# Values in a phase of their own ahead of attention, by seven block products of eight, and output weights from head 13 on

## The chip, the cores and the metric

The kernel runs on one core of one Trainium2 chip. The metric is device time in microseconds (us) for one execution. PE is the matmul engine (TensorE), DVE is VectorE, ACT is ScalarE, POOL is GpSimd, and SP (SyncE) is the engine whose queue issues nearly all DMAs here.

## The reference, cut to what matters

A two-layer encoder trunk over 1024 tokens of width 1024, in float32. Layer 0 mixes tokens with a gated MLP (gMLP) and then has a convolutional feed-forward network. From the residual stream behind it one shared key and value is projected. Layer 1 is chunked attention with 16 heads of 64 against that key and value, again followed by a feed-forward network, and a last normalization.

```python
h = h + gmlp_mixer(rmsnorm(h, a_norm_g[0]), ...)
h = h + conv_ffn(rmsnorm(h, f_norm_g[0]), ...)
kv = rmsnorm(h, kv_norm_g) @ w_kv                 # shared keys and values
k_shared, v_shared = jnp.split(kv, 2, axis=-1)
# chunk_attention: chunks of 64, the own chunk and 8 before it
q = (rmsnorm(h, b_norm_g[0]) @ w_q) * HEAD_DIM ** -0.5
sc = einsum('bqhd,bkhd->bhqk', qb, kb) + bias     # per head, clipped relative positions
p = softmax(where(valid, sc, -1e30))
o = einsum('bhqk,bkhd->bqhd', p, vb)
h = h + o @ w_o
h = h + conv_ffn(rmsnorm(h, f_norm_g[1]), ...)
return rmsnorm(h, final_norm_g)
```

## The kernel before, in words

**Arithmetic.** Every large matmul is done as three: each operand is split into a high part, rounded to the matmul's number format, and a low part, the rest. The products high x high, high x low and low x high are summed (`products`, L174; the three matmuls are on L181, L184 and L188). `split` (L137) makes the parts: ACT casts the high one (L139), DVE or POOL subtracts for the low one (L140). A matmul takes a stationary block of 128x128 and 512 moving columns. `proj` (L169) runs `products` over all 8 blocks of the contraction: 24 matmuls for a result of 128x512.

**Seven products of eight.** The feed-forward networks and the output projection of layer 0 multiply 2x2 blocks with seven block products. Sums of blocks of the weights (S1 to S4) and of the activations (T1 to T4) stand in for single blocks; the tables `LEFT` and `RIGHT` (L302) say which product takes which. `block_sum` (L383) makes a sum, `down` (L913) is the second matmul of a feed-forward network, in 77 steps of 12 matmuls, and adds its results to the residual h.

**Order of work.** PE's order is written out by hand. A clock `tick` (L57) counts matmul time as the code is written, and `put_off` (L66) keeps a piece of work pending until that clock has passed a given number of microseconds, so that it falls between other matmuls. The other engines, SP's queue of DMAs among them, get their order from a scheduler, but for some stretches (in `down` ACT, DVE and SP are by hand up to step 24). An engine works through its own order strictly, and an instruction that waits holds up what stands behind it. Pools of buffers set when a tile can be written again.

**Normalization.** `norm` (L284) is called when `down(0)` has finished a half t of the tokens: `norm_tile` (L257) multiplies a block of h by the row of reciprocal root mean squares into y and splits it into `yh`, `yl`. These are the moving operands of the projections.

**Projections.** The heads come in pairs, 8 pairs p, each 128 features. With the token halves t there are 2 x 24 matmuls for q, k and v of each pair. Pair 0 has its own code right behind `down(0)` (`w2`, `ps2`, and a joint loop on L1128). For pairs 1 to 7 the generator `heads` (L1169) yields after every matmul, in the order q, k, v, and the attention loop takes some matmuls of it per step as fill. `operand` (L1070) moves a result out of PSUM: ACT and DVE make `thi` and `tlo` for q and k. `stage` (L1095) brings them with six DMAs of 64 rows into the operands QE, QS, KM, KS of a head (c is the head's place in its pair; SP queue; L1103). `constant_rows` (L1060) fills the other 64 rows of QE and KM from an input of constants by way of a buffer `e` (DMA L1065, ACT copy L1066). For v, `operand` copies PSUM to `vT`, and `transpose_v` (L1179) turns it on PE (`vtr`, L1182), four 128x128 pieces at a time; ACT and DVE split it into VH and VL, for c=1 by way of a piece that `stage_v` (L1190) moves with two DMAs.

**Attention.** For head hd, `Max` loads the head's bias (L1200), forms the row maxima of scores plus bias from matmuls `mx` (L1210, L1217; DVE reads them with the bias on L1213 and L1219), and its `row` transposes them on PE (`mr`, L1226) and puts them into a row of QE by DMA (L1230). `Head.score` is the score matmul `st` (L1256, L1258), which reads that row. `Head.value` is `po` (L1286 on). The loop has 16 heads of 8 steps. Ahead of it `START` = 58 matmuls of `heads` run, and the first head's maxima are put off by 4.0 us and 0.8 us more for each block, the row by 11.2 us. The number `n` of fill matmuls per step is 12 or 6, for pair 0 (144-58)/16, about 5.4 (3, then 6, in head 13; 5 in heads 14 and 15).

**Output projection.** `output` (L1383) multiplies by w_o; before the change it is used as fill from head 14 on for six of the eight blocks m, and the rest follows after the loop (`open_h("b")`, L1468 on). Sixteen DMAs from ACT's queue save h in `hsave[1]` behind pair 0 (L1138); `hr` reads them back at the end.

## Time and profile before

| | us |
|---|---|
| median of 3 runs | 2132.54 (2130.45 to 2134.04) |
| the profiled execution | 2131.62 |
| its span, first to last instruction | 2129.5 |
| PE busy | 2116.1 |
| DVE busy | 1546.9 |
| ACT busy | 1066.3 |
| POOL busy | 744.6 |

The span is 2.1 us shorter than the execution's own time. Instants below are microseconds from the span's start. `down(0)` ends at 926.9, pair 0's projections fill the stretch to 963, attention runs from there to 1404, and the output projection to 1477. An engine's busy time says how long it had an instruction in hand, not whether something waited for it; the chain of waits tells that. The granted clock of PE was 1.00 in all stretches shown.

### The profile page before, as it was taken

The page shows a single profiled execution, that of the slowest core. Times are in us where ns is not written, and L with a number is a line of the kernel's source. Part 1 is how long each engine was busy: PE and PEld are TensorE (multiplying, and loading weights), DVE is VectorE, ACT ScalarE, POOL GpSimd, SP SyncE. Part 2 cuts the span into 40 slices and gives each one's busy share as a digit, 9 for nine tenths or more (in the row PEclk, how much of TensorE's full clock was granted, in tenths as well). Part 3 has the DMA queues.
Part 4 walks back from the last instruction along what each step waited for, and adds up shares of the span by engine and source line. Part 5 has one row for each costly group of instructions (what it writes and reads, how often), then busy time and mean ns, then how long its engine had stood idle before and what let it go on. Part 6 is the DMA issues. An engine that isn't in the chain of part 4 may idle for free.

```text
span 2129.5 us, 28843 instructions
## 1 busy us (share of the span) xinstructions
PE 2116.1 (99%) x9944; PEld 1771.8 (83%) x9944; DVE 1546.9 (73%) x2313; ACT 1066.3 (50%) x1878; POOL 744.6 (35%) x528
## 2 busy tenths in 40 slices
PE   9999999999999999999999999999999999999998
PEld 8888878888888888878888888888888888888887
DVE  4188789888888857676565665665988888885576
ACT  6333555554445544555555555643645544454443
POOL 1075644332334412054444543421323323342020
PEclk9999999999999999999999999999999999999999
DMA  7267733454445966635555455762244545578653
GB/s 252 80 203 253 242 104 99 139 188 140 172 162 194 299 254 219 238 110 139 132 135 127 127 127 135 186 214 108 79 148 135 187 134 174 164 278 303 213 188 129
DMA packets 181450, 367.86 MB, mean 173 GB/s; under 512 B 42908, under 2 KB 43292, under 8 KB 181304
## 3 DMA queue, kind: packets, MB, share of 16 engines
q1 hardware_dynamic: 177128, 358.47, 52.6%
q10 hardware_dynamic: 4176, 7.55, 1.0%
q8 instruction: 78, 1.28, 0.3%
q14 instruction: 68, 0.56, 0.1%
HBM read 233.12 MB, written 103.40 MB: 158 GB/s over the span
## 4 chain that ended last, share of the span: by engine, by line
PE 93%; DVE 4%; ACT 1%; issue 1%; DMA 0%; POOL 0%; SPq 0%; DVEq 0%; POOLq 0%; ACTq 0%
PE up L995 10%; PE gate L995 10%; PE up L375 7%; PE up L377 7%; PE up L380 7%; PE gate L375 5%; PE gate L380 5%; PE gate L377 5%; PE vps L510 4%; PE qkv L184 4%; PE qkv L181 4%; PE qkv L188 4%; PE ups L181 1%; PE po L1290 1%; PE st L1256 1%; PE po L1288 1%
## 5 line engine op out<-in xcount | busy, mean ns | idle before, releaser
L140 DVE TENSOR_TENSOR wlo<-raw,whi 128x512 fp32r<-128x512 f32 (+1 forms) x395 | 346.5, 883 | 179.7 <-ACT whi L139 179.3
L139 ACT CAST whi<-raw 128x512 fp32r<-128x512 f32 (+1 forms) x395 | 245.1, 623 | 281.1 <-PE gate L995 197.4
L375 PE MATMUL up<-yh,whi 128*128 128x512 f32 x688 | 268.1, 390 | 0.7 <-ACT gate L886 0.6
L377 PE MATMUL up<-yh,wlo 128*128 128x512 f32 x688 | 267.8, 389 | 0.0
L847 POOL TENSOR_TENSOR h<-a 128x512 f32<-128x512 f32 x44 | 82.0, 1864 | 403.3 <-DVE a L839 390.7
L1270 POOL TENSOR_TENSOR pl<-p,ph 128x640 fp32r<-128x640 f32 (+4 forms) x128 | 159.7, 1250 | 173.2 <-ACT ph L1269 128.0
L375 PE MATMUL gate<-th,whi 128*128 128x512 f32 x496 | 192.9, 389 | 0.0
L377 PE MATMUL gate<-th,wlo 128*128 128x512 f32 x496 | 192.9, 389 | 0.0
L380 PE MATMUL up<-yl,whi 128*128 128x512 f32 x688 | 184.2, 389 | 0.0
L375 PEld LDWEIGHTS up<-yh,whi 128*128 128x128 f32 x688 | 129.2, 188 | 28.9 <-ACT gate L886 2.0
L380 PEld LDWEIGHTS up<-yl,whi 128*128 128x128 f32 x688 | 129.1, 188 | 27.3 <-POOL yl L140 0.5
L377 PEld LDWEIGHTS up<-yh,wlo 128*128 128x128 f32 x688 | 129.2, 188 | 26.6
L140 DVE TENSOR_TENSOR yl<-raw,yh 128x512 fp32r<-128x512 f32 x172 | 143.1, 835 | 8.5 <-ACT yh L139 8.1
L184 PE MATMUL qkv<-yh,wlo 128*128 128x512 f32 x336 | 134.3, 400 | 0.0
L380 PE MATMUL gate<-tl,whi 128*128 128x512 f32 x496 | 132.8, 389 | 0.2 <-DVE tl L140 0.2
L181 PE MATMUL qkv<-yh,whi 128*128 128x512 f32 x336 | 132.4, 394 | 0.0
L139 ACT CAST whi<-S 128x512 fp32r<-128x512 f32 x160 | 99.2, 620 | 66.2 <-PE up L380 60.3
L140 DVE TENSOR_TENSOR wlo<-S,whi 128x512 fp32r<-128x512 f32 x160 | 130.6, 817 | 0.0
L995 PE MATMUL up<-yl,whi 128*128 128x512 f32 (+1 forms) x312 | 120.6, 387 | 0.0
L995 PE MATMUL gate<-yh,wlo 128*128 128x512 f32 (+1 forms) x312 | 120.4, 386 | 0.0
L995 PE MATMUL up<-yh,whi 128*128 128x512 f32 (+1 forms) x312 | 120.4, 386 | 0.0
L995 PE MATMUL up<-yh,wlo 128*128 128x512 f32 (+1 forms) x312 | 120.3, 386 | 0.0
(307 smaller groups left out, 5263.7 us busy)
## 6 DMA issues: line engine op xcount, KB each, us to landing
raw<-in_f_win SPq DMA_DIRECT2D x88, 512.0 KB
gT<-h SPq DMA_DIRECT2D x88, 256.0 KB
h<-in_f_wdown SPq DMA_DIRECT2D x44, 512.0 KB
dS<-h SPq DMA_DIRECT2D x88, 256.0 KB
raw<-dS SPq DMA_DIRECT2D x40, 512.0 KB
raw<-gT SPq DMA_DIRECT2D x40, 512.0 KB
gB<-a SPq DMA_DIRECT2D x66, 256.0 KB
raw<-in_f_wdown SPq DMA_DIRECT2D x30, 512.0 KB
```

Of the source, the lines that this page charges most:

```text
L139: behind[S] = S.copy(hi, src)
L140: return eng.tensor_tensor(lo, src, f32(hi), op=ALU.subtract)
L181: nc.tensor.matmul(ps, wh[:, k, :], xs[k][0], start=k == 0, stop=False)
L184: nc.tensor.matmul(ps, wl[:, k, :], xs[k][0], start=False, stop=False)
L188: nc.tensor.matmul(ps, wh[:, k, :], xs[k][1], start=False, stop=k == last)
L375: nc.tensor.matmul(ps, wh[:, k, :], xs[k][0], start=first and k == 0, stop=False, skip_group_check=True)
L377: nc.tensor.matmul(ps, wl[:, k, :], xs[k][0], start=False, stop=False, skip_group_check=True)
L380: nc.tensor.matmul(ps, wh[:, k, :], xs[k][1], start=False, stop=k == 3, skip_group_check=True)
L510: nc.tensor.matmul(ps, a, b, start=k == i == 0, stop=k == KD - 1 and i == 2)
L847: G.tensor_tensor(B[n], x, B.get(y) if isinstance(y, str) else y, op=ALU.subtract)
L995: nc.tensor.matmul(ps[:, cs], w[:, ms], x[:, cs], start=q == i == 0 and p in (1, 6, 5, 4), stop=q == NP - 1 and i == 2, skip_group_check=True)
L1270: marks[2] = G.tensor_tensor(pl[:, :n], pf[:, :n], f32(ph[:, :n]), op=ALU.subtract)
```

## The change

Values no longer take part in the fill. Behind `down(0)` a phase `values()` computes V for all heads with tokens on partitions, by the seven block products in the order 1, 2, 3, 6, 7, 5, 4, each for four token tiles m and four blocks of the contraction, 12 matmuls for a tile. Products 2 and 7 go on in the PSUM bank of products 1 and 6. The weights' sums (`value_sums`) are made on POOL during `down(0)`, at its steps 28, 37, 46 and 55, and go through DRAM (`va`); the gain is applied to them there. `norm` now scales h in place and makes the activations' sums T1 to T4 in place behind it; the T operands are split as they are needed (`tee`). The results are split and stored in DRAM (`vd`), and `stage_v` reads each head's piece, 64 columns, straight into VH and VL, while `vT`, the transposes and `constant_rows` ahead of pair 0 go. The phase stops twice (`yield`) for pair 0's q and k, t=0 behind product 1 and t=1 behind product 3. Their results stay in PSUM until the phase is over; only then come `first`, `stage(0, ...)`, `constant_rows` for c=0 and c=1 (two buffers, tag "o"), and `stage(1, ...)`.

The fill of attention is then only q and k (672 matmuls, `START` = 75 of them ahead of the loop), spread evenly over the 13 x 8 steps of heads 0 to 12. Heads 13 to 15 are filled with the output projection, 4 matmuls a step and 5 in every fourth; blocks m = 2 to 5 are first done for five of the eight k and added to `hr`. The weights w_o are asked for at steps 100 to 116. The put-off of the first maxima is 6.5 + 0.8 b, that of the row 14.0. The stores of h to `hsave[1]` move into `down(0)`. Core of the diff:

```diff
-START = 58
+START = 75
...
-    def norm(h, acc, t, gain, ys):
+    def norm(h, acc, t, X):
...
             def tile_k(k):
-                ys[t][k] = norm_tile(h[k][:, halves[t]], bc, k, gain, npl)
-            for k in range(KD):
-                put_off(0.9 * k, lambda k=k: tile_k(k))
+                y = h[k][:, halves[t]]
+                V.tensor_tensor(y, y, bc, op=ALU.mult)
+                X[f"B{1 + k // 4}{1 + t}"][k % 4] = b = new_y()
+                split(*b, y, V if k % 2 else G)
+
+            def sums(k):
+                (y11, y12), (y21, y22) = [[h[i][:, hs] for hs in halves] for i in (k, k + 4)]
+                V.tensor_tensor(y11, y12, y11, op=ALU.subtract)
+                V.tensor_tensor(y12, y22, y12, op=ALU.subtract)
+                V.tensor_tensor(y22, y22, y11, op=ALU.subtract)
+                G.tensor_tensor(y21, y21, y22, op=ALU.subtract)
...
                 behind["h"] = V.tensor_tensor(x, ps[:, cs], x, op=ALU.add)
+                if not l:
+                    (nc.scalar if t else nc.sync).dma_start(hsave[1][m + 4 * (p in (5, 4)), :, halves[t]], x)
...
+    def value_sums(k):
+        rows = [vs.tile([P, T], F32, tag="vr", name="vr") for _ in range(2)]
+        for j in range(2):
+            nc.sync.dma_start(rows[j].rearrange("p (m c) -> p m c", c=P), value_rows(0, k + 4 * j))
+            c = C_KVG + k + 4 * j
+            G.tensor_tensor(rows[j], rows[j], cc[:, c:c + 1].broadcast_to([P, T]), op=ALU.mult)
+        A = {f"A{n + 1}{j + 1}": rows[j][:, halves[n]] for n in range(2) for j in range(2)}
+        for n in va:
+            nc.sync.dma_start(va[n][k], block_sum(A, n, lambda: vs.tile([P, H], F32, tag="vS", name="vS", bufs=8), G))
...
+    def values():
...
+        def out(n, t, m, src, eng=V):
+            hi, lo = (npl.tile([P, H], F32R, tag="acc", name=a, bufs=4) for a in ("vh", "vl"))
+            split(hi, lo, src, eng)
+            for d, a in zip(vd, (hi, lo)):
+                nc.sync.dma_start(d[4 * t + m, :, halves[n]], f32(a))
...
+            elif p == 5:
+                out(1, 1, m, added(ps, s1[m]), G)
+                out(0, 1, m, added(ps, x[m]))
+            else:
+                out(1, 0, m, added(ps, s1[m]))
...
+        for n, (p, m) in enumerate(steps):
+            if p in (2, 6) and m == 0:
+                yield
+            if todo:
+                weight(*todo.pop(0))
+            if n + 2 < len(steps):
+                tee(*steps[n + 2])
+            if p not in (2, 7):
+                bank[m] = psA("v")
...
+            for k, (xh, xl) in enumerate(operand(p, m)):
+                wh, wl = wv[p, k]
+                for i, (a, b) in enumerate(((xh, wh), (xh, wl), (xl, wh))):
+                    nc.tensor.matmul(bank[m], a, b, start=p not in (2, 7) and k == i == 0, stop=k == 3 and i == 2,
+                                     skip_group_check=True)
+                    tick()
+            whole(p, m, bank[m])
...
+        for t, _ in enumerate(values()):
+            ys[t] = X["B11"] + X["B21"] if t == 0 else X["B12"] + X["B22"]
+            for what in "qk":
+                if t:
+                    ps2[what, 1] = psS("qk")
+                proj(ps2[what, t], w2[what], ys[t])
...
+    for t in range(2):
+        for what in "qk":
+            first(what, t)
+        stage(0, halves[t])
...
-        constant_rows(1, lambda: b2.tile([P, H], F32, tag="o", name="e"))
         for c in range(2):
+            constant_rows(c, lambda: b2.tile([P, H], F32, tag="o", name="e"))
...
-            order = [(p, what) for p in range(1, KD) for what in ("q", "k", "v")]
+            order = [(p, what) for p in range(1, KD) for what in "qk"]
...
+        def stage_v(hd):
+            for dst, a in zip((VH, VL), vd):
+                nc.sync.dma_start(f32(dst[hd % 2][:, :, rows[hd % 2][0]]),
+                                  a[:, :, hd * 64:(hd + 1) * 64].rearrange("b p c -> p b c"))
...
-        stage(1, halves[0])
+        for hs in halves:
+            stage(1, hs)
+        stage_v(0)
         mx = Max(0)
         for b in range(NB):
-            put_off(4.0 + 0.8 * b, lambda b=b: mx.block(b))
-        put_off(11.2, mx.row)
+            put_off(6.5 + 0.8 * b, lambda b=b: mx.block(b))
+        put_off(14.0, mx.row)
...
+            if s < ends:
+                n = left * (s + 1) // ends - left * s // ends
+            else:
+                n = 4 + (s % 4 == 3)
...
+            if i == LAG + 1 and hd + 1 < NH:
+                stage_v(hd + 1)
```

More of the change, by code (lines that the diff above doesn't have):

```diff
@@ L172, in proj, with products @@
             pass
-    def products(ps, w, xs, ks, last):
+    def products(ps, w, xs, ks, last, first=0):
         wh, wl = w
@@ L911, in ffn, with down @@
         return gs, ds
-    def down(l, gs, ds, hold, after):
+    def down(l, gs, ds, hold, after, aside={}):
         wd = f_wdown[l].rearrange("(q e p) c -> p q e c", e=2, p=P)
@@ L1040, in trunk @@
+    raws["ctx"].close()
+    npool_ctx.close()
+    h_ctx.close()
     open_raw(3)
@@ L1383, in output, with load_hr @@
         def output(todo):
-            for m, load, bank in todo:
-                w = load()
+            for m, ks, bank in todo:
                 ps = bank("wo")
-                yield from products(ps, w, os_[0], range(LAST), None)
-                outs.append((m, w, ps))
-        outs, head, waiting, ws = [], None, [], {}
-        loads = [0, 2, 8, 10, 11, 12]
+                yield from products(ps, ws[m], os_[0], ks, ks[-1] if ks[-1] < LAST - 1 else None, ks[0])
+                if ks[-1] < LAST - 1:
+                    V.tensor_tensor(hr[m], ps, hr[m], op=ALU.add)
+                else:
+                    outs[m] = ps
+        def load_hr(i):
+            place = f32(bt.tile([P, T], F32R, tag=("thi", "tlo")[i % 2], name="hr"))
+            for j in range(2):
+                hr[2 * i + j] = place[:, halves[j]]
+                with tc.issue_after(behind["row"].ins):
+                    nc.sync.dma_start(hr[2 * i + j], hsave[1][2 * i + j, :, halves[0]])
+        outs, head, waiting, ws = {}, None, [], {}
+        loads = {100: 2, 102: 3, 106: 4, 109: 5, 112: 0, 116: 1}
+        left = 2 * 6 * KD * LAST - early
+        ends = 13 * NB
         mid, end = {2: (1,), 3: (3,), 4: (5,), 5: (7,)}, {1: (0,), 2: (2,), 3: (4,), 4: (6,)}
```

235 lines of the change are left out of this document (118 added, 117 removed).

## The prediction

> **What bounds the kernel now.** I read the page first: the span, the busy shares and the chain that ended last.
>
> ```profile
> span 2129.5 us, 28843 instructions
> PE 2116.1 (99%) x9944; PEld 1771.8 (83%) x9944; DVE 1546.9 (73%) x2313; ACT 1066.3 (50%) x1878; POOL 744.6 (35%) x528
> PE 93%; DVE 4%; ACT 1%; issue 1%; DMA 0%; POOL 0%; SPq 0%; DVEq 0%; POOLq 0%; ACTq 0%
> ```
>
> PE is busy for 99% of the span and holds 93% of the chain. So a matmul that goes away counts in full, and so does every microsecond in which PE is made to wait. "Mean ns of one" is no price for a matmul, since matmuls overlap. The price is the pitch from start to start, which an unbroken piece of the chain of waits gives (72 matmuls of 128x512), and for the small transposes the timeline of PE (start, length, instruction):
>
> ```profile
> 55.66 16.35 PE vps L510 x72
> ...
> 962.66 1.03 PE L1182 MATMUL vtr<-ident,vT 128*128 128x128 f32 x8
> 963.45 0.47 PE L181 MATMUL qkv<-yh,whi 128*128 128x512 f32 x1
> ...
> 967.89 0.22 PE L1210 MATMUL mx<-km,qe 128*128 128x128 f32 x1
> ...
> 975.49 0.27 PE L1226 MATMUL mr<-ident,mb 128*8 128x128 f32 x1
> ...
> 978.82 0.28 PE L1256 MATMUL st<-qe,km 128*128 128x256 f32 x1
> ```
>
> 16.35/72 = 0.227 us for a 128x512 matmul; (963.45 - 962.66)/8 = 0.099 us for a transpose. The last three rows time the entry to attention, used below: first maximum product (mx) at 967.89, its row transpose (mr) at 975.49, first score (st) at 978.82.
>
> The busy time by stage (the end of down(0), pair 0's projections, the entry, heads 0, 1, 13 and 15) shows how much room the other engines have:
>
> ```profile
> core 0: us, PE busy (x) PEld busy (x) DVE busy (x) ACT busy (x) POOL busy (x), PEclk, DMA share, GB/s
> 873.00:926.90 53.90, 53.90 (x241) 44.39 (x240) 37.62 (x54) 28.11 (x51) 13.29 (x9) 1.00 0.47 156
> 926.90:963.00 36.10, 35.34 (x160) 28.71 (x159) 22.25 (x35) 18.61 (x35) 16.59 (x15) 1.00 0.50 147
> 963.00:979.00 16.00, 16.00 (x82) 13.38 (x81) 11.86 (x33) 5.85 (x12) 2.75 (x2) 1.00 0.74 196
> 979.00:1000.50 21.50, 20.89 (x114) 17.96 (x114) 13.63 (x38) 13.38 (x29) 13.63 (x11) 1.00 0.26 65
> 1000.50:1022.20 21.70, 21.70 (x125) 19.17 (x124) 11.71 (x37) 13.19 (x30) 12.84 (x12) 1.00 0.44 109
> 1338.00:1358.00 20.00, 20.00 (x115) 17.68 (x115) 10.63 (x34) 12.81 (x27) 10.03 (x9) 1.00 0.88 238
> 1381.00:1404.00 23.00, 22.25 (x118) 19.10 (x118) 19.10 (x29) 16.03 (x34) 10.23 (x9) 1.00 0.59 186
> ```
>
> The entry (963 to 979) costs PE nothing today: 16.00 of 16.00 us busy.
>
> **What goes.** The V projections of pairs 1 to 7 are part of three groups of 336, and the transposes are one of 64:
>
> ```profile
> L188 PE MATMUL qkv<-yl,whi 128*128 128x512 f32 x336 | 95.1, 396 | 0.0
> L1182 PE MATMUL vtr<-ident,vT 128*128 128x128 f32 x64 | 9.5, 273 | 0.4 <-ACT vT L1092 0.4
> ```
>
> A third of 3 x 336 is V, 336 matmuls, and pair 0 has 48 more: 384. The phase does 7 x 4 x 12 = 336. So 48 matmuls go, 48 x 0.227 = 10.9 us, and 64 transposes, 64 x 0.099 = 6.3 us: **-17.2 us**. With them go vT's copies and splits from PSUM, on engines with room.
>
> **What moves at no price, and its cover.** 597 of the 672 q,k fills are spread over 104 steps, 5.7 a step; heads 0 and 1 hold 5.4 a step today, and head 1 has PE busy for 21.70 of 21.70 us. Heads 13 to 15 get 4.25 output matmuls a step; head 13 now averages 4.5 (3, then 6) without a gap, and head 15 loses 0.75 us at 5. If that cover fails I expect up to 1 us a head, 3 us in all; I take 0. The 16 stores of h go from ACT's queue to SP and ACT within down(0), behind the adds that make x; PE waits for none of them. The row that each head's value needs from DRAM is asked for in the head before, about 13 us ahead (five of eight steps of a 21.7 us head). The wait of PE at the second half's statistics (36.10 - 35.34 = 0.76 us) may stay or go; I count nothing.
>
> **The block sums in down(0): 8 gain products and 16 sums on POOL.** Prices: the sums of down's own h, and a gain product beside DVE splits (POOL's timeline, then DVE's):
>
> ```profile
> L847 POOL TENSOR_TENSOR h<-a 128x512 f32<-128x512 f32 x44 | 82.0, 1864 | 403.3 <-DVE a L839 390.7
> ...
> 976.25 4.20 POOL L159 TENSOR_TENSOR raw<-raw,cc 128x1024 f32<-128x1024 f32 x2 [17.35 <-DMA raw<-in_w_q]
> ...
> 962.61 0.69 DVE L140 TENSOR_TENSOR wlo<-raw,whi 128x512 fp32r<-128x512 f32 x1 [1.50 <-ACT whi L139]
> ...
> 976.35 2.35 DVE L140 TENSOR_TENSOR wlo<-raw,whi 128x512 fp32r<-128x512 f32 x1 [0.91 <-ACT whi L139]
> ...
> 979.22 1.78 DVE L140 TENSOR_TENSOR wlo<-raw,whi 128x512 fp32r<-128x512 f32 x1
> ```
>
> POOL gets 16 x 1.86 + 8 x 2.10 = 46.6 us more. A split that takes 0.69 us alone took 2.35 and 1.78 beside POOL: 2.75 us lost in 4.20 of POOL, so 46.6 us could cost DVE 30.5. They stand in 36 of down's steps of 12 matmuls, 98 us; DVE's slack there is 1 - 37.62/53.90 = 30%, 29.6 us. It just fits. I take 0 here, and +1 (0 to 3) for the step p=3 of the phase, where eight DVE ops and the POOL halves stand between two uses of a bank.
>
> **The new wait: the entry to attention.** Before, constant rows, bias and half of pair 0's staging go out on SP while PE still projects pair 0. SP's order there (e: constant rows; km, qe, qs, ks: staging of q and k; thi, tlo: their halves):
>
> ```order
> L1065 DMA e<-in_consts 64x512 x2
> L1200 DMA bias<-in_bias 128x512 x2
> L1103 DMA km_8618<-thi 64x512
> L1103 DMA qe_8616<-thi 64x512
> L1065 DMA e<-in_consts 64x512 x2
> L1103 DMA qs_8617<-thi 64x512
> L1103 DMA qe_8302<-thi 64x512
> ```
>
> After the change, the same place of SP:
>
> ```order
> L1182 DMA e<-in_consts 64x512 x2
> L1213 DMA km_9394<-thi 64x512
> L1213 DMA qe_9392<-thi 64x512
> L1182 DMA e<-in_consts 64x512 x2
> L1213 DMA qs_9393<-thi 64x512
> L1213 DMA qs_9393<-tlo 64x512
> L1182 DMA e<-in_consts 64x512 x2
> L1213 DMA ks_9395<-tlo 64x512
> L1213 DMA ks_9395<-thi 64x512
> L1182 DMA e<-in_consts 64x512 x2
> ```
>
> Ahead of it now stand 24 stores of V pieces and the 12 stagings of head 0; behind it six stagings, two loads of V, and only then the bias. And it is all late, since ACT makes thi only behind the last V split (vh: V's high half, c: the sum it is cast from):
>
> ```order
> L139 CAST vh_9259<-c_9257 128x512 [waits DMAHW7_49,DVE_49,Activation_49]
> L139 CAST vh_9280<-c_9278 128x512 [waits DMAHW1_49,DVE_49,Activation_49]
> L1199 ACTIVATE thi_9354<-qk_8386 128x512
> L1202 CAST thi_9358<-qk_8387 128x512 [waits PE_49]
> L1199 ACTIVATE thi_9354<-qk_8800 128x512
> L1202 CAST thi_9358<-qk_8825 128x512
> ```
>
> What moved: pair 0's eviction went from beside its projections to behind the whole phase. On PE, before:
>
> ```order
> L188 MATMUL qkv<-yl,whi 128x512 x3
> L1210 MATMUL mx<-km_8304,qe_8302 128x128
> L188 MATMUL qkv<-yl,whi 128x512 x3
> L1210 MATMUL mx<-km_8304,qe_8302 128x256
> L188 MATMUL qkv<-yl,whi 128x512 x2
> ```
>
> and after:
>
> ```order
> L181 MATMUL qkv<-yh,whi 128x512
> L1286 MATMUL mx<-km_9352,qe_9350 128x128
> L184 MATMUL qkv<-yh,wlo 128x512
> L181 MATMUL qkv<-yh,whi 128x512
> L184 MATMUL qkv<-yh,wlo 128x512
> L1286 MATMUL mx<-km_9352,qe_9350 128x256
> ```
>
> The first mx now stands 31 fills behind the last V matmul (before, 19 behind the transposes), and st 75 fills behind it instead of 58. The prices, from SP's timeline, ACT's and DVE's:
>
> ```profile
> 952.25 1.28 SPq L1065 DMA_DIRECT2D e<-in_consts  x2
> 953.57 1.27 SPq L1200 DMA_DIRECT2D bias<-in_bias  x2
> ...
> 957.84 1.14 SPq L1065 DMA_DIRECT2D e<-in_consts  x2
> ...
> 966.00 0.59 SPq L1103 DMA_DIRECT2D km<-thi  x1
> ...
> 969.20 0.59 SPq L1103 DMA_DIRECT2D ks<-thi  x1
> ...
> 970.66 0.67 SPq L1192 DMA_DIRECT2D vl<-vlo  x1
> ...
> 998.99 0.39 SPq L1200 DMA_DIRECT2D bias<-in_bias  x1
> ...
> 960.63 1.33 ACT L1066 CAST km<-e 64x512 fp32r<-64x512 f32 x2 [0.34 <-DMA e<-in_consts]
> ...
> 968.14 0.29 DVE L1213 CUSTOM_DVE_ANT_0 junk<-mx,bias 128x128 f32<-128x128 f32 x1 [1.84 <-DMA km<-thi]
> ...
> 975.21 0.23 DVE L1221 SCALAR_TENSOR_TENSOR mb<-ma,cc,mb 128x6 f32<-128x6 f32 x1
> ```
>
> One issue: (969.20 - 966.00)/5 = 0.64 us. One constant row: 957.84 to 960.63, 2.8 us, and a cast of 0.6, 3.4 in all. The maxima on DVE: 968.14 to 975.44, 7.3 us; from mr to st 3.3.
>
> Let T be the end of the last V matmul. Its sum, cast and split: 0.7 + 0.6, T+1.3. Then SP issues 14 rows up to the last staging of head 0, 9.0 us: the first constant row leaves at X = T+10.3 at best. The V pieces have four buffers; a cast, a store and its landing are some 4.5 us for a pair of pieces, two pairs at once, so 2.2 us a pair where p=5 makes one each 1.36 us: eight pairs fall 6.9 us behind and p=4 (2.72 us a pair) gives 2 back. X is T+10 to T+15; I take 12.5. The four pairs of constant rows share two buffers, so each waits for the cast of the last: 3 x 3.4 = 10.2. Two rows, six stagings, two loads: 10 x 0.64 = 6.4, and the bias leaves at X+16.6, lands at +19.4 (2.8, as a constant row), DVE is through at +26.7, st can start at X+30. PE gets there by itself at 75 x 0.227, and 2.2 for the mx (before: 978.82 - 963.45 - 58 x 0.227): T+19.2. **Wait: X + 10.8, +23.3 us (21 to 26).** Behind the waiting mx stand all fills, in PE's own order.
>
> The sum: -17.2 + 23.3 + 1.0 = +7.1 on the profiled execution's 2131.62 us (span and 2.1 us around it). That execution lies 0.92 below the median of the runs, 2132.54, so I forecast **2139.6 us**; its own range is -17.2 + 21 + 0 to -17.2 + 26 + 3, 2136 to 2144.
>
> The Trainium skill, DMA: Bandwidth & Descriptors, "Issuing engines are not separate DMA queues", says the time a sequencer takes to start a DMA is usually small beside the DMA itself. The rows above say 0.64 beside 2.8, which is small for one and not for 24 in a row; by the rule the sum would be that of the second rival.
>
> **Rivals.**
> 1. *The issues are shorter in quiet* (0.39 us, as the bias at 998.99): X = T+1.3+5.5, then 10.2 + 3.9 + 2.8 + 7.3 + 3.3 = T+34.3; wait 15.1, 2132.5 - 17.2 + 15.1 + 1.0 = 2131. For it: DMA was 74% busy when 0.64 was seen. Against it: the constant rows at 952.25 also took 0.64 each.
> 2. *Issues cost nothing, only landings do* (SP is done before its rows are needed): 1.3 + 10.2 + 2.8 + 7.3 + 3.3 = T+24.9, wait 5.7, 2132.5 - 17.2 + 5.7 + 1.0 = 2122. Against it: between 966.00 and 969.20 SP had six stagings in a row and each took its 0.64.
> 3. *Slower still: DVE becomes the bound of down(0).* If a DVE op beside POOL always loses POOL's whole time, DVE loses 46.6 us against 29.6 of slack: 17 us more, 2157; half of it 2148. It decides once DVE's busy time in a step passes 2.72 us. For it: 2.35 against 0.69. Against it: 2.75 lost in 4.20, not all. That it would lose all of it is what the Trainium skill, SBUF — State Buffer, "Who interferes with whom", says of an op with two SBUF inputs beside a GpSimd op that reads SBUF: whoever comes second blocks fully.
>
> That the work doesn't go isn't open: PE's order has 48 matmuls and 64 transposes less.
>
> **Chances.** Forecast 0.48; rival 1 0.18; rival 2 0.20; rival 3 0.08; 0.06 for a full gain with hardly a wait, below 2120. About 0.2% (4.3 us) is what a measurement can tell from no change: 2128.3 to 2136.8. Forecast: 0.46 slower, 0.02 same. Rival 1: 0.04 faster, 0.11 same, 0.03 slower. Rival 2 and the rest: faster. Rival 3: slower. Faster 0.30, same 0.13, slower 0.57. The range of 8 in 10 runs from 2120 (0.06 below) to 2148 (0.08 above).
>
> **What would show it.** Right: the last V matmul to the first st takes about 42 us with PE idle for some 23 of them, first in front of mx (releaser ACT km<-e), then of the later mx (DVE junk, behind DMA bias), then of st (DMA qe<-mr); elsewhere 17 us less of PE. Wrong: PE busy through the entry (rival 2), or gaps in down(0) with DVE as releaser (rival 3); a pitch other than 0.227 in the phase would upset the gain.

## The result and the profile after

| | kernel before | changed kernel |
|---|---|---|
| median of 4 runs beside each other (range) | 2131.81 us | 2197.49 us (2194.22 to 2200.13) |
| ratio, 95% interval | | 1.0306 [1.0288, 1.0324] |
| profiled execution: time, span | 2131.62, 2129.5 us | 2200.13, 2198.4 us |

The change makes the kernel slower by 3.1%. The forecast, 2139.6 us, had the sign; 2197.49 lies far above its range (2120 to 2148). In the experiments two kernels had one execution each that was far slower (row_step5 7525.49 us, best_hr 3525.64); their ratios and ranges are of the other three. The first rows of the changed kernel's page, to be held against those of before in the prediction:

```profile
span 2198.4 us, 28916 instructions
PE 2124.1 (97%) x9832; PEld 1770.0 (81%) x9832; DVE 1591.9 (72%) x2354; ACT 1075.4 (49%) x1879; POOL 802.0 (36%) x560
PE 83%; DMA 6%; DVE 6%; issue 2%; POOL 1%; SPq 1%; ACT 1%; DVEq 0%; POOLq 0%; ACTq 0%
```

112 matmuls went (9944 to 9832), as forecast, but PE is idle for 2198.4 - 2124.1 = 74.3 us where it was idle for 13.4, and DMA, which had 0% of the chain, now has 6%. Busy time by stage shows where (length, then PE busy; the stages are the second half of down(0), the value phase, the entry, heads 0 to 12, heads 13 to 15, the end of the output projection):

```profile
core 0: us, PE busy (x) PEld busy (x) DVE busy (x) ACT busy (x) POOL busy (x), PEclk, DMA share, GB/s
744.00:931.00 187.00, 182.39 (x793) 148.50 (x792) 146.83 (x172) 92.56 (x165) 74.84 (x44) 0.99 0.79 269
931.00:1037.40 106.40, 105.86 (x469) 87.17 (x468) 79.73 (x108) 44.09 (x77) 39.22 (x27) 1.00 0.38 129
1037.40:1087.00 49.60, 24.33 (x90) 19.11 (x90) 14.37 (x35) 11.14 (x20) 9.30 (x10) 0.69 0.70 186
1087.00:1386.00 299.00, 285.84 (x1529) 247.53 (x1527) 173.02 (x499) 179.78 (x376) 155.40 (x135) 0.98 0.61 149
1386.00:1464.00 78.00, 68.08 (x354) 58.73 (x355) 46.86 (x115) 43.86 (x93) 32.57 (x29) 0.96 0.65 181
1464.00:1486.00 22.00, 14.43 (x57) 11.27 (x56) 16.18 (x28) 8.17 (x15) 2.91 (x3) 0.80 0.39 130
```

The value phase is as forecast: PE waits 106.40 - 105.86 = 0.54 us in all of it. Idle time is in five places: 4.6 us in down(0), 25.3 at the entry, 13.2 in heads 0 to 12, 9.9 in heads 13 to 15, 7.6 behind the last score. The clock column tells of a second cost: 0.69 at the entry, where it was 1.00 before. Busy time doesn't count that. So I worked out for each stage the excess: over all neighbouring matmuls, the distance from start to start, less the median distance that the same form has in the kernel before. It holds idle time and lowered clock alike (us, in profiled executions; heads 0 to 12 run from the first score to the row transpose mr of head 13; "rest" is up to 700 us, the value phase and all behind the output projection):

| kernel | down(0) from 700 us | entry | heads 0-12 | heads 13-15 | behind the last score | rest | sum |
|---|---|---|---|---|---|---|---|
| before | 0.2 | 0.2 | 6.8 | 2.7 | 0.1 | 11.6 | 21.6 |
| changed | 8.4 | 30.9 | 26.6 | 15.1 | 10.9 | 16.6 | 108.4 |
| difference | +8.2 | +30.7 | +19.8 | +12.4 | +10.8 | +5.0 | +86.8 |

86.8 less the 17.2 of the work that went is 69.6; the spans differ by 68.9. So nothing is missing from the sum. The profiled execution of the change is the slowest of its four, 2.6 us above the median, so profiles differ by a little more than medians. Of the 5.0 in the rest, 4.0 lie behind the output projection, and no run asks for their cause. What made each place is the question of the experiments.

**The entry** went in the order that the prediction had. The chain of the changed kernel (start, length, what):

```profile
1024.93 12.47 PE v L1139 x55
...
1050.08 4.09 DMA e<-in_consts
...
1062.41 0.49 SPq L1182
...
1068.15 4.38 DMA bias<-in_bias
1072.76 0.29 DVE junk L1289
...
1082.81 0.27 PE mr L1302
```

T is 1024.93 + 12.47 = 1037.40. The first constant row leaves at T+12.7 (12.5 was taken), the last at 1062.41, the bias at 1068.15; the first score starts at 1087.03. PE's waits, in total, times and longest:

```profile
PE mx L1286 <- DMA e<-in_consts: 13.8, 1, 13.8
PE mx L1293 <- DVE mb L1289: 11.2, 4, 9.7
PE st L1332 <- DMA qe<-mr: 7.6, 5, 2.8
PE st L1332 <- DVE mb L1289: 7.0, 4, 2.1
PE wo L184 <- DVE wlo L140: 4.0, 1, 4.0
...
PE wo L181 <- DVE h L1569: 3.6, 1, 3.6
PE po L1362 <- DVE o L1391: 3.2, 1, 3.2
PE up L992 <- DVE wlo L140: 2.6, 1, 2.6
```

The longest waits of the first two rows, 13.8 and 9.7, are the entry; those for qe and mb are the heads, those of wo the tail, po is head 13, and the last row is down(0).

### The profile page after: what moved, and what is told of

Same layout as the page of the kernel before. It is cut to its first block, busy times and chain, and to the rows that moved or that the text cites. A ratio compares the mean times of both kernels' runs of the same rounds, so it can differ in the third digit from the quotient of the medians.

```text
span 2198.4 us, 28916 instructions
## 1 busy us (share of the span) xinstructions
PE 2124.1 (97%) x9832; PEld 1770.0 (81%) x9832; DVE 1591.9 (72%) x2354; ACT 1075.4 (49%) x1879; POOL 802.0 (36%) x560
## 4 chain that ended last, share of the span: by engine, by line
PE 83%; DMA 6%; DVE 6%; issue 2%; POOL 1%; SPq 1%; ACT 1%; DVEq 0%; POOLq 0%; ACTq 0%
PE gate L992 8%; PE up L992 8%; PE up L370 7%; PE up L368 7%; PE up L373 7%; PE gate L373 5%; PE gate L370 5%; PE gate L368 5%; PE vps L503 4%; PE v L1139 3%; PE qkv L188 2%; PE qkv L181 2%; PE qkv L184 2%; PE ups L181 1%; PE ups L184 1%
## 5 line engine op out<-in xcount | busy, mean ns | idle before, releaser
L140 DVE TENSOR_TENSOR wlo<-raw,whi 128x512 fp32r<-128x512 f32 x380 | 349.2, 925 | 139.6 <-ACT whi L139 139.3
L139 ACT CAST whi<-raw 128x512 fp32r<-128x512 f32 x380 | 235.2, 622 | 286.9 <-PE gate L992 180.0
L140 DVE TENSOR_TENSOR yl<-raw,yh 128x512 fp32r<-128x512 f32 x172 | 152.4, 888 | 9.0 <-ACT yh L139 9.0
L139 ACT CAST yh<-raw 128x512 fp32r<-128x512 f32 x190 | 115.1, 616 | 13.5 <-DMA raw<-gB 8.8
L992 PE MATMUL gate<-yl,whi 128*128 128x512 f32 (+1 forms) x312 | 120.8, 387 | 0.0
```

What stands on the lines that cost most here:

```text
L139: behind[S] = S.copy(hi, src)
L140: return eng.tensor_tensor(lo, src, f32(hi), op=ALU.subtract)
L992: nc.tensor.matmul(ps[:, cs], w[:, ms], x[:, cs], start=q == i == 0 and p in (1, 6, 5, 4), stop=q == NP - 1 and i == 2, skip_group_check=True)
```

## The experiments

The theory: five causes in five places (the entry's chain; POOL's value sums in down(0); the reads of V in heads 0 to 12; the loads of the residual ahead of head 14's bias; matmuls spent early that used to cover the last head's division). The rival: one cause, say the order of the last heads or the crowd of transfers, of which the rest are echoes.

**1. The reads of V.** stage_v reads each head's V as 64 columns of 4 bytes, twice a head:

```diff
         def stage_v(hd):
+            if hd > 1:
+                return
```

> It leaves out the loads of V for heads 2 to 15 (they use the V of heads 0 and 1). Theory A, the loads of V in pieces of 256 bytes from DRAM make the small DMAs beside them land late (the maxima's row to qe, the denominators to few): the 20 us that heads 0 to 12 lose over before fall to under 8, and the kernel is 12 to 20 us faster than the changed one, about 2180. Theory B, the row is simply asked for too late for a fill of 5.7 a step: 0 to 4 us faster.

2185.87 us (2184.04 to 2190.36), ratio 1.0259 [1.0244, 1.0274]: 11.6 less than the change. Heads 0 to 12 lost 14.3 instead of 26.6, everything ahead of them the same. The chain in head 8 of the changed kernel, and the clock behind it:

```profile
1283.73 4.65 DMA few<-den
...
1288.52 0.42 DVE junk L1289
...
1289.01 0.44 PE st L1332
```

```profile
1290.00:1295.00 5.00, 4.46 (x13) 3.38 (x12) 3.69 (x10) 1.87 (x4) 0.78 (x2) 0.50 0.55 158
```

The denominators take 4.65 us to come back from DRAM. In DVE's order the maxima (junk) stand behind them, and the scores behind those. PE waits 2 us, and then works at a clock of 0.50. DVE's waits for few between 1085 and 1400 us:

```profile
DVE few L1414 <- DMA few<-den: 7.2, 4, 3.0
```

Without V's reads no such wait is left there. These heads scatter, so one pair of profiles says little; over all kernels of this study they lost 16.7 to 30.8 us with V's reads (15 profiles, mean 24.1) and 12.8 to 18.9 without (4 profiles, mean 14.9). The reads cost about 9 us on these means, though the two ranges overlap.

**2. Bytes or pieces?** The same bytes and as many issues, but in pieces of 2 KB and from DRAM to DRAM:

```diff
+            if hd > 1:
+                for place, a in zip(spare, vd):
+                    nc.sync.dma_start(place[hd], a[hd % 8, :, 0:H])
+                return
```

> As in the run without the loads of V from head 2 on, but each such load is replaced by one of the same bytes, from the same place in DRAM to other DRAM, in pieces of 2 KB; the heads use the V of heads 0 and 1. If it is the 256-byte pieces that make the others late: as without the loads, 2184 to 2188. If it is the bytes and the issues on SP: as the changed kernel, 2194 to 2199.

2191.20 us, 1.0286 [1.0269, 1.0303], between the two forecasts. But the run doesn't answer the question. The scheduler put all 28 stand-ins ahead of attention, whose first score starts at 1094.9 us here (issues, then the instants of the first and the last):

```profile
L1270 SPq DMA_DIRECT2D spare<-vhi x14: 475/564/1354, 968.5 to 1083.2; - x14
L1270 SPq DMA_DIRECT2D spare<-vlo x14: 469/525/927, 973.7 to 1084.6; - x14
```

So none runs beside heads 0 to 12, and the 12.8 us that these lose are a second case of a kernel without V's reads. The stand-ins show at the entry instead: among them the last store of V's pieces leaves at 1053.87 instead of 1041.50, the first constant row at T+19.2 instead of T+12.7, and the entry loses 36.9 us, 6 more than in the change. Whether the cost of V's reads is their bytes, SP's time for the issues or the 256-byte pieces stays open. The changed kernel's profile shows the pieces in its line on packets:

```profile
DMA packets 220812, 391.99 MB, mean 178 GB/s; under 512 B 60764, under 2 KB 75484, under 8 KB 220664
```

Without the reads (v_once) 31644 are under 512 bytes. The kernel before had 42908; its V went in such pieces too, but from SBUF to SBUF. The Trainium skill, DMA: Bandwidth & Descriptors, "Why small descriptors are slow (HBM only)", says that small pieces are slow when DRAM is at one end, and that transfers from SBUF to SBUF don't suffer. No run here shows it.

**3. The sums in down(0).** In the changed kernel POOL's 8 gain products and 16 sums do not lie over 98 us. They stand from 745.90 to 801, with few gaps. POOL, DVE and PE at the place where PE waits:

```profile
775.53 2.10 POOL L1047 TENSOR_TENSOR vr<-vr,cc 128x1024 f32<-128x1024 f32 x1 [0.20 <-DMA vr<-in_w_kv]
...
779.42 1.62 POOL L383 TENSOR_TENSOR vS<-vS,vr 128x512 f32<-128x512 f32 x1
...
784.41 5.43 POOL L960 TENSOR_TENSOR h<-h,u 128x512 f32<-128x512 f32 x4
```

```profile
775.80 2.38 DVE L140 TENSOR_TENSOR wlo<-raw,whi 128x512 fp32r<-128x512 f32 x1
...
779.81 1.78 DVE L140 TENSOR_TENSOR wlo<-raw,whi 128x512 fp32r<-128x512 f32 x1
...
785.73 0.69 DVE L958 TENSOR_TENSOR u<-up,s 128x512 f32<-128x512 f32 x1 [1.24 <-POOL h L960]
```

```profile
788.76 0.50 PE L992 MATMUL up<-yh,wlo 128*128 128x512 f32 x1 [2.58 <-DVE wlo L140]
790.44 0.50 PE L992 MATMUL up<-yl,whi 128*128 128x512 f32 x1 [1.17 <-DVE yl L140]
...
791.39 0.63 PE L992 MATMUL gate<-yl,whi 128*128 128x512 f32 x1
```

A DVE split of 0.69 us takes 2.38 beside a POOL operation of 2.10, and 1.78 beside one of 1.62: each ends about 0.55 us behind the POOL operation. POOL's own adds to h come late, for which DVE waits too. The busy time of DVE (the third pair of numbers) in this stretch, before and after:

```profile
745.90:801.20 55.30, 55.30 (x246) 45.80 (x245) 30.01 (x45) 25.17 (x46) 5.50 (x4) 1.00 0.66 241
745.90:801.20 55.30, 51.06 (x212) 40.22 (x210) 50.64 (x35) 21.73 (x39) 49.83 (x28) 0.97 1.01 343
```

Two ways to move the sums, then the sums left out:

```diff
-{28 + 9 * k: lambda k=k: value_sums(k) for k in range(4)}
+{48 + 7 * k: lambda k=k: value_sums(k) for k in range(4)}
```

> The sums of the value weights are asked for at steps 48, 55, 62 and 69 of down(0) in place of 28, 37, 46 and 55. Theory C, the 7 us lost at 785 to 795 come from POOL's run of sums in front of its adds to h, which DVE and then PE wait for: they go, 8 us faster, if the sums now run behind product 7. Rival: they are lost to the traffic of loads there, then 0 to 3 us.

2193.48 us, 1.0294 [1.0270, 1.0319]. No effect: POOL still ran the sums from 748 to 804, and down(0) lost 9.1. The step at which the code asks for them doesn't set when they run.

```diff
+            with tc.issue_after(behind["h"].ins):
-            G.tensor_tensor(rows[j], rows[j], cc[:, c:c + 1].broadcast_to([P, T]), op=ALU.mult)
+                G.tensor_tensor(rows[j], rows[j], cc[:, c:c + 1].broadcast_to([P, T]), op=ALU.mult)
...
+{40 + 8 * k: lambda k=k: value_sums(k) for k in range(4)}
```

> The gain products of the value sums are held back behind the adds to h that follow product 2 of down(0), which ends at step 33, and asked for at steps 40 to 64. The scheduler of the earlier run had put the sums at 748 to 804 all the same; now they should stand at 805 on. Theory C (POOL's sums ahead of its adds to h, DVE slowed by them): the waits at 785 to 795 go, 7 to 9 us faster, less what the sums cost beside product 7. Rival: the same loss, later.

2190.91 us, 1.0276 [1.0261, 1.0292]. Again none: 745 to 800, 8.5 us lost. Yet the medians of these two lie 4.0 and 6.6 us under the change's. So a median that is lower by less than about 7 us doesn't speak for an edit here; the loss in the place that was edited has to show it.

```diff
-            G.tensor_tensor(rows[j], rows[j], cc[:, c:c + 1].broadcast_to([P, T]), op=ALU.mult)
...
-            nc.sync.dma_start(va[n][k], block_sum(A, n, lambda: vs.tile([P, H], F32, tag="vS", name="vS", bufs=8), G))
+            nc.sync.dma_start(va[n][k], A[f"A{1 + (n > 'S2')}{1 + (n in ('S2', 'S4'))}"])
```

> It leaves out POOL's gain products and block sums for the value weights (the stores to DRAM take the loaded blocks as they are, so V is wrong); loads, stores and the rest stay. The scheduler had put those 47 us of POOL work at 745 to 801 of down(0) whatever step asked for them. Theory C, they slow DVE's splits to POOL's pace and PE runs out of operands: the 8.5 us lost in the second half of down(0) fall under 1, the kernel is 6 to 10 us faster. Rival, the loads of 4 MB beside down's own are what is late: 0 to 3 us.

2186.05 us (2182.31 to 2196.66), 1.0264 [1.0235, 1.0292]. The stretch that had 182.39 us busy of 187:

```profile
744.00:931.00 187.00, 187.00 (x828) 154.62 (x828) 128.56 (x184) 94.31 (x168) 31.90 (x21) 1.00 0.76 268
```

PE is busy throughout and the excess is 0.2, as before the change. So POOL's work is the cause of these 8.2 us. The loads and the stores stayed, so they are not.

**4. The entry.** Constant rows rounded into DRAM ahead of the value phase and sent straight into place, and the bias asked for ahead of head 1's staging:

```diff
+        for j in range(4):
+            nc.sync.dma_start(e, consts[:, P + j * H:P + j * H + H])
+            S.copy(r, e)
+            nc.sync.dma_start(rounded[:, j * H:j * H + H], f32(r))
...
-                S.copy(tl[oth, hs], e[oth])
+            nc.sync.dma_start(f32(tl[oth, :]), rounded[oth, off:off + T])
...
+        mx = Max(0)
         for hs in halves:
             stage(1, hs)
```

> The constant rows are rounded into DRAM ahead of the phase and go straight into qe and km, and the first bias is asked for ahead of head 1's staging. Theory D, the entry's wait is the chain of issues and landings on SP: without three round trips (10 us) and 8 issues ahead of the bias the entry's 31 us fall to 10 to 14, and the kernel is 17 to 21 us faster, about 2178. Rival, PE waits there for the V pieces and the evictions themselves: under 8 us faster.

2190.93 us (2184.89 to 2195.28), 1.0281 [1.0256, 1.0307]. The entry lost 13.5 instead of 30.9: the chain of constant rows, issues and bias is what PE waited for. Of the 17 us only 6.6 reached the median; in the profiled run heads 0 to 12 lost 4 more and down(0) 3 more than in the change. The 4 lie within the scatter of these heads. The 3 are a new wait, at the end of down(0) (about 914 us), where the change has none:

```profile
PE pm L249 <- DVE acc L238: 2.6, 1, 2.6
```

All five kernels that have both this edit and the value sums wait there, 2.4 to 3.1 us. So the edit takes back part of what it gives.

```diff
-START = 75
+START = 110
...
-            put_off(6.5 + 0.8 * b, lambda b=b: mx.block(b))
-        put_off(14.0, mx.row)
+            put_off(14.0 + 0.8 * b, lambda b=b: mx.block(b))
+        put_off(22.0, mx.row)
```

> 110 fills in place of 75 ahead of the first score, the first maxima put off by 14 in place of 6.5 us and the row by 22 in place of 14; the steps of heads 0 to 12 then have 5.4 fills in place of 5.7. Theory D, the entry waits for a chain that runs by itself: 35 matmuls, 7.9 us, move into the wait, the entry's 31 us fall to 21 to 24, and what the heads lose grows by 0 to 4, so 4 to 9 us faster. Rival, the entry's chain moves along with the fills (evictions stand in it): no gain.

2187.96 us (2186.69 to 2188.68), 1.0264 [1.0248, 1.0279]. The entry lost 20.7 instead of 30.9, and the median fell by 9.5. Heads 0 to 12 lost 30.2, and 30.0 in all3_start below; both are near the upper end of the scatter, so that cover spent here is lacking there is likely, but not shown.

**5. The row of each head.** Earlier in the head, then on another queue:

```diff
-                if i == (6 if p < LAST - 1 else 5):
-                    put_off(0.5 if p < LAST - 1 else 2.0, mx.row)
+                if i == 5:
+                    put_off(2.0, mx.row)
```

> The maxima's row is sent about 1.3 us earlier in heads 0 to 12 (step 5 + 2.0 us in place of step 6 + 0.5 us). Theory B, the lead of the row is what is short: the waits of the first score (1.97, 0.67, 1.93, 0.25, 2.80 us) go, and with them the slow clock behind them, 8 to 14 us faster. Theory A, DVE stands in front of a late few and PE behind DVE, and landings are late by traffic: the waits of 2 us in the middle of heads (1289, 1338, 1385) stay, 3 to 7 us faster.

Ratio 1.0278 [1.0261, 1.0295] (2187.49 to 2193.08 us), heads 0 to 12 21.1.

```diff
-                behind["row"] = nc.sync.dma_start(f32(QE[self.c][row:row + 1, :]), f32(mr))
+                behind["row"] = nc.scalar.dma_start(f32(QE[self.c][row:row + 1, :]), f32(mr))
```

> The maxima's row goes out on ACT's queue in place of SP's. If SP's order holds it up (in head 13 the cast ended at 1390.0 and SP sent it at 1393.8, behind a wait for rden): the 2.80 us there go, and 1 us in head 3: 3 to 7 us faster. If the landing among other traffic is what is long: 0 to 2 us.

2190.78 us, 1.0281 [1.0266, 1.0297], heads 0 to 12 16.7. Both look like a gain, but kernels that leave these heads alone lost from 18.5 (the next one) to 30.8 (sums_late) there in their one profile, and with the same row on ACT's queue all3 (below) lost 23.6. I count neither as shown.

**6. Behind the last score.** The changed kernel's PE, and DVE at that place:

```profile
1477.53 0.77 PE L181 MATMUL wo<-yh,whi 128*128 128x512 f32 x1 [3.60 <-DVE h L1569]
1482.26 0.79 PE L184 MATMUL wo<-yh,wlo 128*128 128x512 f32 x1 [3.97 <-DVE wlo L140]
```

```profile
1471.15 3.39 DVE L1404 RECIPROCAL den<-den 128x128 f32<-128x128 f32 x4
...
1476.69 3.68 DVE L1569 TENSOR_TENSOR h<-wo,hr 128x512 f32<-128x512 f32 x6
1480.29 3.06 DVE L140 TENSOR_TENSOR wlo<-raw,whi 128x1024 fp32r<-128x1024 f32 x2
```

DVE divides the last head; the adds that free the output's banks and the next weight split stand behind that. Before, 53 output matmuls (12 us) were left over behind the last value product; now 18 are (4 us). First fewer matmuls a step, then block 5 wholly behind the loop and half as many matmuls ahead of the last values:

```diff
-                n = 4 + (s % 4 == 3)
+                n = 3 + (s % 4 == 3)
```

> Heads 13 to 15 take 3.25 output matmuls a step in place of 4.25, so that 24 more are left for behind the loop. If the 7.6 us of waits behind the last score are cover that the change used up (DVE's reciprocals of the last pair and the last two weights stand ahead of the output's adds): they fall to about 2, and the heads' own waits grow by less, 3 to 6 us faster. If DVE is late whatever PE does: no gain, or slower by the waits in the heads.

2197.82 us (2191.64 to 2198.95), 1.0307 [1.0291, 1.0323]: nothing. The matmuls saved ran ahead of the last values, not behind them; 10.1 us lost.

```diff
-        fill = output([(m, range(LAST - 2, LAST), psS) for m in (2, 3, 4, 5)])
+        fill = output([(m, range(LAST - 2, LAST), psS) for m in (2, 3, 4)] + [(5, range(LAST), psS)])
         for h0, b in waiting:
-            for _ in range(12):
+            for _ in range(6):
```

> Block m=5 of the output is wholly done behind the loop, heads 13 to 15 take 3.25 output matmuls a step, and 6 in place of 12 of them stand ahead of each of the last two values: about 27 matmuls (6 us) more stand behind the last value product, where the changed kernel has 18. If the waits of 3.6 and 4.0 us there are that missing cover: they fall to 1 to 3 us together, 4 to 7 us faster, with the clock's part. If the weights or h come late: no gain.

2187.44 us (2186.73 to 2191.28), 1.0266 [1.0250, 1.0281]. Only one wait is left there, 1.9 us in front of wo with DVE's split (wlo) as releaser, and the excess is 2.3 instead of 10.9 (heads 13 to 15 lost 17.9 instead of 15.1).

**7. Heads 13 to 15.** The residual's rows 1 and 2 (four issues), asked for behind head 14's bias instead of ahead of it:

```diff
-                for i2 in (1, 2):
-                    load_hr(i2)
...
                 mx = Max(hd + 1)
+                if s == ends:
+                    for i2 in (1, 2):
+                        load_hr(i2)
```

> At the start of head 13 the four loads of h (1 MB) go out behind head 14's bias in place of ahead of it. The bias landed 8 us after its issue there and DVE stood 2.7 us in front of it, PE 3.2 us behind DVE: these go, 3 to 6 us faster. Rival, the waits in head 13 come from the osave loads and the row that SP sends late: under 2 us.

2191.44 us, 1.0276 [1.0259, 1.0293]; heads 13 to 15 lost 13.4 instead of 15.1. Little, but the scheduler moved only one of the four issues behind the bias; three still went out ahead of it.

**8. Do the parts add?** Entry, row on ACT's queue and tail together; then with the gain products on ACT; then with V's reads and the sums left out; then with START = 110:

```diff
 (all3_act)
-            G.tensor_tensor(rows[j], rows[j], cc[:, c:c + 1].broadcast_to([P, T]), op=ALU.mult)
+            S.activation(rows[j], rows[j], AF.Copy, scale=cc[:, c:c + 1])
```

> Three of the edits together: constant rows rounded early and sent straight in with the bias ahead of head 1's staging, each head's row on ACT's queue, and block 5 of the output projection wholly behind the loop. Theory that the losses are separate stages that add: by the stages measured one edit at a time (entry 30.9 to 13.5, heads 0 to 12 26.6 to 16.7, tail 10.9 to 2.3) 36 us less than the change, about 2162. Rival, that a wait taken out of one stage mostly comes back in the next, so that only the medians' gains stay (6.6, 6.7 and 10.1, of which some is scatter): 2175 or more.

> The same three and the eight gain products of the value sums on ACT instead of POOL, which takes 16.8 of 46.6 us from POOL in down(0). If DVE loses what POOL takes, in proportion, the 8.5 us of down(0) fall to 5.4 and the time is 3 us under that of the three alone. If the loss is that the sums stand ahead of POOL's adds to h, whatever their number, it stays at 8.5.

> The three edits, with V's loads left out from head 2 on and the gain products and sums of V's weights left out (work is missing, so only the time counts). It asks whether the causes found account for the whole loss. If they do, down(0) loses 0.2, heads 0 to 12 about 13, the entry 13.5, the tail 2.3: total 61 us over the pitch, 2150. The forecast's own gain of 17.2 would show in full only if heads 0 to 15 lost no more than the 9.5 us that they lose before the change; that would give 2134. Anything above 2160 means a cause is still missing.

> The three edits, gain products on ACT, and 110 fills instead of 75 ahead of the first score, with the maxima 7.5 and 8 us later in the order of the code. If the entry is a wait for data that a later start simply covers, its 13.5 us fall to about 4 (35 x 0.227 = 7.9, and less slow clock behind the wait), and heads 0 to 12, which then have fewer fills, give back some 4: 2155 to 2160. Rival: the fills taken from the heads are missed there as much as they cover here, as in the change with 110 alone (26.6 to 30.2), and the time is that of the three with ACT.

| kernel | us (range) | ratio, 95% interval | down(0) | entry | heads 0-12 | heads 13-15 | behind the last score | sum |
|---|---|---|---|---|---|---|---|---|
| all3 | 2179.33 (2176.83 to 2181.88) | 1.0217 [1.0200, 1.0234] | 14.7 | 13.7 | 23.6 | 17.4 | 2.1 | 89.7 |
| all3_act | 2173.41 (2169.21 to 2177.78) | 1.0194 [1.0173, 1.0214] | 8.3 | 13.8 | 22.2 | 14.3 | 2.1 | 77.7 |
| all3_bare | 2162.50 (2159.45 to 2165.22) | 1.0142 [1.0127, 1.0157] | 2.7 | 13.3 | 18.9 | 19.4 | 2.2 | 72.4 |
| all3_start | 2182.12 (2174.49 to 2188.46) | 1.0233 [1.0208, 1.0258] | 9.7 | 13.2 | 30.0 | 21.1 | 2.1 | 90.8 |

Entry and tail add: 13.7 and 2.1, as alone. But the entry's new wait comes along; at about 915 us it makes 6.8 of the 14.7 in down(0). The heads don't add: with 2179 all3 lies nearer to the rival's 2175 than to 2162. all3_act is 6 us below it, with intervals that overlap. In its down(0) the loss at the sums (740 to 850 us) is 3.7, where it is 8.1 in all3 and in the change; all3_start and best_hr, which have the gain products on ACT too, lose 4.6 and 4.4 there, and the 13 kernels with all of this work on POOL lose 8.0 to 8.8. So moving these 16.8 of POOL's 46.6 us halves the loss at the sums; what is left of the 8.3 is the entry's new wait. START = 110 covers nothing more once the constant rows come early (13.2 for 13.8) and heads 0 to 12 lose some 8 us more in this one profile. all3_bare should have come to 2150 if the causes were all; 12 us were left, in both groups of heads. The largest wait, in head 13:

```profile
1365.74 8.49 DMA bias<-in_bias
...
1374.91 0.41 DVE junk L1296
...
1375.99 0.48 PE po L1369
```

Head 14's bias takes 8.49 us to land instead of the 4.38 of the entry, and DVE holds a value product's bank (o) behind it. So the same edit of the residual's loads was put into all3_act (best_hr) and all3_bare (bare_hr):

> The three edits, gain products on ACT, and rows 1 and 2 of the second half's residual (eight transfers of h) loaded behind head 14's bias instead of ahead of it. In the four kernels before, the bias of head 14 left behind three of these transfers, took up to 8.5 us, and PE then waited 3.2 to 5.8 us in front of a value product of head 13, with DVE as releaser. If the order behind SP is what made the bias late, that wait goes and heads 13 to 15 fall from 14.3 to about 8: 2167. Rival: the bias is late because the transfer engines are full at that place, then some other small transfer of head 13 or 14 is late in its stead and the time stays at 2173.

> The same move of the residual's loads in the kernel without V's loads from head 2 on and without the value sums (work is missing). It was 2162.5 with 19.4 us lost in heads 13 to 15. If the bias is the cause, these fall to about 10 and the time to 2153; what is then left over the kernel before is the entry (13), and heads that are shorter by the fills of V that went (22 us for one instead of 28 on the mean) with the same trips to DRAM and back in each.

best_hr: 1.0188 [1.0167, 1.0208] (2168.87 to 2175.90 us), heads 13 to 15 16.3 us. bare_hr: 2160.33 us (2152.43 to 2161.84), 1.0124 [1.0104, 1.0143], heads 13 to 15 15.6. Again the order is hardly changed; in best_hr three of the four issues still stand ahead of the bias, in bare_hr all four:

```profile
1371.89 1.43 SPq L1478 DMA_DIRECT2D hr<-hsave  x3
1373.41 0.38 SPq L1282 DMA_DIRECT2D bias<-in_bias  x1
```

So what the order is worth is not tested. DVE's wait for this bias did get shorter (0.3 us in best_hr after 3.5 in all3_act, 1.9 in bare_hr after 4.3 in all3_bare), and other waits stand in its stead: in best_hr PE waits 3.7 us in front of mr, in bare_hr 3.4 in front of po. In best_hr heads 13 to 15 lose 16.3 after 14.3, so the wait for the bias alone doesn't make their loss, which is what the rival says; whether full transfer engines do stays open. No version comes near the kernel before.

## Why the prediction was wrong

- **"-17.2 us" for what goes**: right. 112 matmuls less, and the value phase kept its pitch (excess 1.2 with 1.5 before). The +1.0 for its step p=3 did not come.
- **"+23.3 us" for the entry**: right in mechanism, place and first term (X = T+12.7 for T+12.5, which was picked from T+10 to T+15, so part of that is luck), mis-sized: 25.3 us idle and 30.7 with the clock. From X to the first score (1087.03) are 36.95 us instead of 30: the constant rows' chain took 12.3 (10.2 taken), the issues up to the bias 5.7 (6.4), its landing 4.4 (2.8), the maxima 10.3 (7.3), the row 4.2 (3.3). Rivals 1 and 2 fell: SP's issues kept their 0.6 us. (Eight pairs of V pieces fall 6.7 us behind by the numbers given, not 6.9; nothing hangs on it.)
- **"I take 0" for the sums in down(0)**: wrong, +8.2. The failed step is "They stand in 36 of down's steps of 12 matmuls, 98 us", with "It just fits". They ran in 55 us, and DVE had 25.3 us free there (30.01 of 55.30 busy before) for a cost that the prediction itself put at 30.5. It is rival 3 at half its price. The Trainium skill's rule that is cited there, that whoever comes second blocks, fits the trace: a split that starts after the POOL operation ends about 0.55 us behind it. It loses what is left of the operation (1.69 of 2.10 us, 1.09 of 1.62), not all of it.
- **"What moves at no price"**: wrong, +19.8 in heads 0 to 12, +12.4 in heads 13 to 15 and +10.8 behind the last score. The first failed at "is asked for in the head before, about 13 us ahead": that counts when it is asked for, not when it lands, nor what is in the way. V's reads are about 9 of the 19.8. What makes the rest stays open. One would look to the length of a head, 22 us without V's fills instead of 28 (24.7 and 32.1 by turns before), with trips to DRAM and back that stay as long. But the traces speak against a price that every head pays: in v_once heads 9 to 11 take 22.0 us each, from first score to first score, and lose 0.4 each, no more than the shorter heads of before (22.6 us, 0.4). The second failed at "up to 1 us a head"; what makes it stays open. The wait for head 14's bias is not enough, since it went to 0.3 us in best_hr and the loss stayed. The third was in no step: I costed 4.25 output matmuls a step and never asked what the matmuls taken from the end had been covering. tail_cover shows that it is this.
- **The clock** was in no step. Every wait was priced at its length.

## What to carry to other kernels

When work is cut out, list what it was hiding, stage by stage: the fills of a head, the leftovers at a tail and the engines beside a dense stretch all paid for the 17 us here. Place helper work by where it will run, not by the step that asks for it, and count an engine's slack in that stretch alone. The same holds for an experiment: look in its trace where the edited operations ran before reading its time, since in six runs here they had not moved, or not as far as asked. Price a small transfer by its landing among the others of its time, and a wait of PE by its length and the lower clock that can follow it.

## What the runs showed of the hardware that was not expected

The clock falls after some short waits, and not after others. At the entry (same columns as above):

```profile
1060.00:1065.00 5.00, 3.44 (x11) 2.45 (x9) 0.29 (x1) 1.85 (x3) 1.03 (x2) 0.50 0.56 163
```

After 13.8 us of waiting the clock is 0.50 and stays there for all the work between the two waits. That agrees with the rule of the Trainium skill, TensorE: Matmul & The Clock Gate, Part 1, by which an idle window of about 3.4 us halves the clock and as long a busy one restores it. But here waits of 2.58 and 1.17 us in down(0), with one matmul between them, were followed by matmuls at a distance of 0.43 us for 3 us (791.39 above), and a single wait of 2.06 us at 1289.01 by a clock of 0.50. Nor is about 2 us a bound. The stretches behind waits of 1.97, 2.00 and 2.80 us in the heads:

```profile
1155.88:1159.70 3.82, 3.82 (x13) 3.33 (x14) 1.92 (x3) 2.30 (x5) 3.68 (x5) 0.55 1.02 229
1338.60:1344.00 5.40, 5.40 (x27) 4.33 (x28) 4.11 (x12) 2.74 (x7) 1.04 (x2) 1.00 0.51 138
1396.70:1402.00 5.30, 5.30 (x31) 4.84 (x32) 4.56 (x6) 4.31 (x9) 1.68 (x2) 1.00 0.86 251
```

The shortest of them was followed by a lowered clock, the longest was not. What decides it, the traces don't tell.

Of the 86.8 us of excess, 74.3 - 13.4 = 60.9 are idle time. In seven stretches the clock was 0.50, and PE was busy for 38.74 us in them; at half the clock that is some 19 us lost (an estimate, half of 38.74). The other 7 are in neither; most likely they are gaps that busy time hides, since a matmul counts as busy for 0.39 us while the next starts 0.227 us after it.
